# Transposing v and h in a decoder layer: TensorE identity products or transposing DMAs with ScalarE plane copies

## The chip, the cores and the metric

The kernel runs on one core of a Trainium2 chip. The metric is the device time of one execution in microseconds (us); a kernel's time is the median of its runs. A profile is one further execution, recorded by the hardware profiler; durations of single instructions come from it.

The engines of the core are named as the profile names them: PE (TensorE, matrix products), PEld (its weight loads), DVE (VectorE), ACT (ScalarE), POOL (GpSimd) and SP (SyncE, which here issues nearly all transfers). Each engine works through its own instructions in a fixed order. SBUF is the on-chip memory with 128 partitions, PSUM the accumulators that PE writes.

## The reference

One layer of a decoder trunk over 1024 prompt tokens and 8 sample tokens, with 1024 features, all in fp32:

```python
xn = _rmsnorm(x, pre_g)
u, v, z_a, x_b, z_b, g_a, g_b = split(xn @ w_in)
vn = _layernorm(gelu(v), ln_g, ln_b)                  # per token, over the features
y_a = gelu(u) * _chunk_spatial_mix(vn, w_s, b_s) * silu(z_a)   # mixes the 128 tokens of a chunk
y_b = pool_branch(x_b) * silu(z_b)
m = sigmoid(g_a) * (y_a @ w_pa) + sigmoid(g_b) * (y_b @ w_pb)
h = h + _rmsnorm(m @ w_out, post_g)
e = p @ w_ple
gate = sigmoid(_rmsnorm(h, ple_in_g) @ w_pg)
h = h + _rmsnorm(gate * e, ple_out_g)
```

The change touches two places. v comes out of its product with the features on the partitions, and the layer norm and the mix want tokens there. h comes out of the product with W_out with the tokens on the partitions, and the product with W_pg, which contracts over features, wants features there.

## The kernel before

**Products.** Each large product runs in four pairs of 128-row blocks, and each pair as seven smaller products, P1 to P7, over quarters of the operands (Strassen and Winograd's scheme; only pair 0 of v is done as four plain steps). The operands on the right are quarters and sums of quarters: B11, B21 and B22 are quarters, T1 to T4 sums. The names in the trace put the operand's letter ahead (`xB11h`, `woT1h`, `wgB22l`), and `h` and `l` at the end are the two parts of an fp32 value, since every fp32 product is three matmuls: high by high, high by low, low by high. ACT makes the high part by a copy (`split`), DVE the low part by a subtraction. A product of one quarter is 12 matmuls of 512 columns in PSUM. There are three PSUM regions of two banks for these sums (`acc`, `acct`) and two single banks for all else (`vt`, `pht`, `mix`). P5 and P3 use the same region: P3 adds onto what P5 left there, so P3 can't begin before DVE has read P5's sum.

**Stages** in the order of time: v, the gate g_A, u and z_a, x_b and z_b with the pooling, the gate g_B, the products with W_pa and W_pb, the product with W_out (`outsteps`, whose tiles are `mw`, `wo...` and `h`), and the product with W_pg (`gatesteps`, whose tiles are `hw`, `wg...` and `ge`).

**Order.** The program records all operations first (`Planner.take`) with a due time counted back from the matmul that needs them, and an estimate of each one's duration (`Planner.duration`). `Planner.order` then works out one fixed order for each engine, and `play` issues it. So all instructions after the first few carry one line number, that of `play` (L293, and L297 after the change), and they are told apart by their tiles. `at(step, f)` hangs an operation to a step of seven; a larger step number means later.

**v.** `v_turn` transposes two token blocks of a pair of v at a time: four products with the identity on PE into a bank `vt`, from which ACT takes the gelu and writes it into `big`, an SBUF tile with tokens on the partitions, adding up each row on the way (`vsums`). There are 64 such 128 x 128 transposes and 8 small ones for the 8 sample tokens. The layer norm (`ln_stats`, `ln_apply`) and the mix (`v_split`, `spatial`) follow in the stage of g_A.

**h.** `out_finish(t)` scales a block of 128 tokens by its norm and adds the layer's input by an accumulating DMA of POOL, then stores it. `gate_norm(t)` takes the sum of squares (ACT), the root (POOL), and multiplies h by it (DVE) into `hn`. `gate_input(t)` transposes `hn` by eight products with the identity into two banks `pht`, and eight ACT copies take them into `big`, each scaled by its feature's gain `ple_in`. There are 64 such transposes. The products with W_pg then read `big` as the left operand (`hw`, `hs`).

**W_pg** is prepared during the stage of x_b and z_b: `column_steps` and `column_sums` load its row blocks and store the sums of quarters to DRAM (`wglow`, `wghigh`, `wgT4`, `wgB22`); the plain quarters B11 and B21 are loaded later from the weight itself.

Of the kernel before, what the change touches and what calls it, by code (L numbers as in the profile page):

```python
# [8 lines left out]
F32 = mybir.dt.float32  # L9
F32R = mybir.dt.float32r  # L10
BF16 = mybir.dt.bfloat16
AF = mybir.ActivationFunctionType
ALU = mybir.AluOpType

P = 128
# [39 lines left out]
class Planner:  # L55
# [25 lines left out]
    def space(self, ap):  # L81

        dims, start = list(ap.ap), ap.offset
        if "DRAM" in str(ap.space):
            row = ap.tensor.shape[-1]
            first, start = divmod(start, row)
            rows = sum(s // row * (n - 1) for s, n in dims if s >= row)
            return (ap.tensor.name, first, first + rows + 1,
                    ((start, start + sum(s * (n - 1) for s, n in dims if s < row) + 1),))
        row, parts = dims[0]  # L90
        first, start = divmod(start, row)
        pieces = [(start, start + 1)]
# [35 lines left out]
    def duration(self, engine, method, out, reads, kwargs):  # L128
# [9 lines left out]
        if engine == "scalar":  # L138
            return max(0.09 + n * 0.00086, 0.26 if n > 1 else 0) + (0.2 if kwargs.get("accum_out") is not None else 0)
        return 0.1 + n * 0.0008 if method == "memset" else 1.0  # L140

    def take(self, engine, method, args, kwargs):
# [14 lines left out]
        if method == "dma_start":  # L157
            op.busy, op.moved = 1.0 if engine == "gpsimd" else 0.45, writes[0].size() * 4e-6
# [141 lines left out]
def hybrid_step(  # L300
# [82 lines left out]
    def root(part, n=P):  # L383

        t, r = sm("ms"), sm("rstd")
# [470 lines left out]
    S = NB  # L856
    xop = Operand("x")
# [7 lines left out]

    def v_turn(out, pair, ts):

        if ts == [S]:
# [3 lines left out]
            places = [(S, ps[:NS, : 2 * P], NS)]  # L872
        else:
            ps = bank("vt").rearrange("p (t c) -> p t c", t=2)
# [3 lines left out]
            places = [(t, ps[:, i], P) for i, t in enumerate(ts)]  # L878
        for t, src, n in places:
            nc.scalar.activation(out=vtok(t)[:n, 2 * pair * P : (2 * pair + 2) * P], in_=src,  # L880
                                 func=AF.Gelu_apprx_tanh, accum_out=vsums[:n, t, pair : pair + 1])

    class V(User):
        turns = [[0, 1], [2, 3], [4, 5], [6, 7], [S]]
# [113 lines left out]
    wgcut = {what: dram.tile([HALF, D], F32, tag="wg" + what, name="wg" + what) for what in ('T4', 'B22')}  # L998
    kept["h"] = dram.tile([T, D], F32, tag="h", name="h")
# [262 lines left out]
    for i, u in enumerate(vusers):  # L1262

        nxt = vsteps[1][3:] if i == 0 else (vsteps[i + 1][1:] if i + 1 < NPAIR else gasteps[0][0:])
        if i == 0:
            nxt = vsteps[1][2:]
        for s, ts in zip(nxt, V.turns):
            at(s, lambda u=u, i=i, ts=ts: v_turn(u.out, i, ts))
# [53 lines left out]
    rows = lambda t: NS if t == S else P  # L1322
# [4 lines left out]
    def column_sums(key, src, b):  # L1327
# [25 lines left out]
    column_steps("wg", w_pg, [(bflow[9 + 7 * i], bflow[12 + 7 * i]) for i in range(4)])  # L1353
# [12 lines left out]
    h_of, parts, hn_of, samples = {}, {}, {}, {}  # L1366
# [36 lines left out]

    def gate_norm(t):

        r = rows(t)
        h = h_of.pop(t)
        hn = hn_of[t] = slot("hn", (P, D))
        rs = rstd([square_sum(h[:r], r, scratch=hn)], r)
        nc.vector.tensor_scalar_mul(hn[:r], h[:r], rs[:r])  # L1410

    def gate_input(t):

        hn = hn_of.pop(t)
        if t == S:
            samples["h"] = sample_stationary(hn, NB, gvec[:, 2 * NB :])
# [296 lines left out]
```

## Time and profile before

| | before |
|---|---|
| time, median of 3 runs | 1001.62 us (1001.23 to 1002.43) |
| span of the profiled execution | 1002.0 us |
| DVE busy | 800.1 us (80%) in 1241 instructions |
| ACT busy | 490.0 us (49%) in 891 instructions |
| POOL busy | 73.7 us (7%) in 162 instructions |
| mean granted clock of TensorE | 0.996 |

The profile has no other time of its execution than the span, which stands within the range of the three runs. A row of a group reads: line, engine, operation, out<-in by the program's names (numbers left out), shapes, count | busy time, mean duration in ns of one | idle time of the engine ahead of them and what ended most of it. A row of the timeline reads: start in us, duration, engine, operation, names, count, and in brackets the idle time ahead of it with its releaser. Consecutive instructions of an engine overlap in these durations, so the cost of one in a row of many is the distance between two starts. A row of the windows gives the busy time of PE, PEld, DVE, ACT and POOL in a stretch of time, then the granted clock, the share of the 16 DMA engines, and GB/s.

### The profile page before, as it was taken

How to read it: one execution, taken by the hardware profiler on the slowest of the kernel's cores; microseconds unless marked ns; L12 is line 12 of the kernel's file. 1: busy time of each engine (PE TensorE's matmuls, PEld its weight loads, DVE VectorE, ACT ScalarE, POOL GpSimd, SP SyncE). 2: the span in 40 equal slices, each digit the busy share in tenths (PEclk: the TensorE clock that was granted, in tenths of full speed). 3: DMA queues.
4: the chain of work that ended last, by engine and by line, in shares of the span. 5: the costliest groups of instructions: out<-in, count | busy, mean ns of one | idle time of the engine just before them, and what ended most of it. 6: DMA issues, size and time to landing. Idle time of an engine off the chain costs nothing.

```text
span 1002.0 us, 16159 instructions
## 1 busy us (share of the span) xinstructions
PE 989.1 (99%) x6200; PEld 889.8 (89%) x6200; DVE 800.1 (80%) x1241; ACT 490.0 (49%) x891; POOL 73.7 (7%) x162
## 2 busy tenths in 40 slices
PE   8999999999999999999999999999999999999996
PEld 7889999999999999999999999999999988888885
DVE  5985448877788788788898887697799798779796
ACT  7664356556434343233433343552353365677653
POOL 2200001000000000000000100000000002312111
PEclk9999999999999999999999999999999999999998
DMA  9231214222364345637544166884573553389546
GB/s 353 117 121 43 84 43 129 85 85 86 101 235 169 127 167 183 210 127 252 200 158 143 61 222 244 266 305 148 199 268 107 177 201 71 80 275 364 160 109 188
DMA packets 87330, 166.95 MB, mean 167 GB/s; under 512 B 7614, under 2 KB 47598, under 8 KB 87245
## 3 DMA queue, kind: packets, MB, share of 16 engines
q1 hardware_dynamic: 84885, 158.01, 45.3%
q0 software_dynamic: 2048, 7.37, 4.3%
q8 instruction: 49, 0.80, 0.3%
q10 hardware_dynamic: 320, 0.54, 0.2%
q14 instruction: 28, 0.23, 0.1%
HBM read 114.59 MB, written 51.77 MB: 166 GB/s over the span
## 4 chain that ended last, share of the span: by engine, by line
PE 97%; DVE 1%; POOL 0%; issue 0%; ACT 0%; POOLq 0%; DVEq 0%
PE acc L293 71%; PE acct L293 15%; PE accm L293 2%; PE e L293 2%; PE sps L293 2%; PE mix L293 1%; PE vt L293 1%; PE pst L293 1%; PE pht L293 1%; PE warm L293 1%; DVE sv L293 0%; DVE ge L293 0%; PE smix L293 0%; PE state L293 0%; DVE welo L293 0%
## 5 line engine op out<-in xcount | busy, mean ns | idle before, releaser
L293 DVE TENSOR_TENSOR u<-acc,u 128x520 f32<-128x520 f32 (+1 forms) x90 | 62.5, 695 | 36.5 <-PE acc L293 35.0
L293 POOL TENSOR_TENSOR rstd<-ms,mhalf 128x1 f32<-128x1 f32 (+1 forms) x45 | 38.2, 851 | 204.8 <-DVE ms L293 182.5
L293 POOL MEMSET u<- 128x8 f32 x35 | 3.5, 105 | 556.1 <-PE acc L293 242.5
L293 ACT ACTIVATE u<-acc 128x512 f32<-128x512 f32 x39 | 23.2, 596 | 33.4 <-PE acc L293 33.1
L293 ACT ACTIVATE paw<-pas 128x512 fp32r<-128x512 f32 x16 | 10.0, 627 | 30.0 <-DVE pas L293 24.8
L293 ACT ACTIVATE pbw<-pbs 128x512 fp32r<-128x512 f32 x16 | 10.0, 629 | 29.1 <-DVE pbs L293 25.9
L293 DVE TENSOR_TENSOR big<-big 128x1024 f32<-128x1024 f32 (+4 forms) x20 | 23.6, 1215 | 0.0
L293 ACT ACTIVATE big<-vt 128x256 f32<-128x256 f32 x32 | 11.9, 380 | 21.4 <-PE vt L293 21.4
L293 ACT ACTIVATE big<-pht,gvec 128x128 f32<-128x128 f32 x64 | 18.0, 381 | 8.0 <-PE pht L293 8.0
L293 ACT ACTIVATE big<-mix 128x256 f32<-128x256 f32 x32 | 12.1, 383 | 19.0 <-PE mix L293 18.6
L293 PE MATMUL accm<-qh,wpoolw 128*128 128x260 f32 (+1 forms) x96 | 21.0, 320 | 0.0
L293 ACT ACT_TABLE_LOAD x13 | 16.7, 1283 | 4.6 <-PE acc L293 3.6
L293 DVE TENSOR_TENSOR v<-acc,u 128x520 f32<-128x520 f32 (+1 forms) x9 | 6.3, 697 | 14.9 <-PE acc L293 14.8
L293 DVE TENSOR_TENSOR acc<-acc,u 128x512 f32<-128x512 f32 (+1 forms) x16 | 11.1, 697 | 8.7 <-PE acc L293 8.7
L293 ACT ACTIVATE gbw<-gbs 128x512 fp32r<-128x512 f32 x16 | 10.0, 624 | 16.4 <-DVE gbs L293 13.8
L293 ACT ACTIVATE zaw<-zas 128x512 fp32r<-128x512 f32 x16 | 10.0, 628 | 14.9 <-DVE zas L293 10.6
L293 ACT ACTIVATE zbw<-zbs 128x512 fp32r<-128x512 f32 x16 | 10.1, 630 | 14.6 <-DVE zbs L293 7.3
L293 PEld LDWEIGHTS accm<-qh,wpoolw 128*128 128x128 f32 x96 | 15.5, 188 | 1.9
L293 DVE TENSOR_TENSOR big<-mix,big 128x256 f32<-128x256 f32 x32 | 13.2, 421 | 4.4 <-ACT big L293 3.5
L293 ACT ACTIVATE uw<-us 128x512 fp32r<-128x512 f32 x16 | 9.8, 627 | 13.7 <-DVE us L293 7.2
L293 ACT ACTIVATE zbw<-zbraw 128x512 fp32r<-128x512 f32 x12 | 7.5, 626 | 18.2 <-DMA zbraw<-in_w_in_dram 9.2
L293 ACT ACTIVATE gb<-gb 128x1032 f32<-128x1032 f32 (+1 forms) x8 | 6.8, 854 | 18.8 <-DVE gb L293 18.8
(687 smaller groups left out, 3629.8 us busy)
## 6 DMA issues: line engine op xcount, KB each, us to landing
ga<-ga SPq DMA_DIRECT2D x16, 516.0 KB
gb<-gb SPq DMA_DIRECT2D x16, 516.0 KB
ya<-za SPq DMA_DIRECT2D x8, 516.0 KB
yb<-zb SPq DMA_DIRECT2D x8, 516.0 KB
x<-in_x_prompt_dram SPq DMA_DIRECT2D x8, 512.0 KB
vraw<-in_w_in_dram SPq DMA_DIRECT2D x8, 512.0 KB
e<-e SPq DMA_DIRECT2D x8, 512.0 KB
garaw<-in_w_in_dram SPq DMA_DIRECT2D x8, 512.0 KB
```

The lines of the kernel that those rows point to most:

```text
L293: getattr(getattr(self.nc, e), method)(*args, **kwargs)
```

## The change

The 64 transposes of v and the 64 of h on PE go; only those of the sample tokens stay.

**v.** `v_planes` takes the two 16-bit halves of each fp32 value of a block apart: two ACT copies (one for the low halves, one for the high ones) write them into a tile `vw` of 16-bit words, all low halves of a row first, then all high ones. A transposing DMA of SP writes `vw` back into the slot of `v`, turned in 128 x 128 blocks of words. `v_join` puts the halves together again, two ACT copies for each block, each for four token blocks, into `big`. `v_turn` then takes the gelu from `big` into `big`.

**h.** `gate_norm` no longer multiplies h by the root. It takes the sum of squares (its squares go into `big`, where they are not used), keeps the root in a column of `vsums` (`rin`), and sends raw h through the same steps: two ACT copies into `hw`, one transposing DMA into the slot of h. `gate_input` joins by two ACT copies. The root enters later as the scale of the sigmoid in `gated`, and the gain `ple_in` goes into W_pg: `column_sums` scales its row blocks on ACT (8 copies of 128 x 1024) and stores their left halves to DRAM (`wgleft`), from which B11 and B21 are then loaded.

The layer norm's steps are hung two steps later, those of W_pg's columns one step earlier. The planner gets durations for the 16-bit copies and handles regions in bytes. GpSimd takes no part in the transposing.

```diff
+    def v_planes(out, pair):
+        for m in range(2):
+            words, v = slot("vw", (P, 2, SEQ), U16), out[m][:, :SEQ].bitcast(U16)
+            for w in range(2):
+                nc.scalar.activation(out=words[:, w], in_=v.rearrange("p (t w) -> p w t", w=2)[:, w], func=AF.Copy)
+            nc.sync.dma_start_transpose(out=v.rearrange("p (k c) -> p k c", c=P),
+                                        in_=words.rearrange("p w t -> p (w t)"))
+
+    def v_join(out, pair, m):
+        c = 2 * (2 * pair + m) * P
+        for j in range(2):
+            ts = slice(4 * j, 4 * j + 4)
+            nc.scalar.activation(out=big.bitcast(U16)[:, ts, c : c + 2 * P].rearrange("p t (c w) -> p t c w", w=2),
+                                 in_=out[m][:, :SEQ].bitcast(U16).rearrange("p (w t c) -> p t c w", w=2, c=P)[:, ts],
+                                 func=AF.Copy)
...
-            for i, t in enumerate(ts):
-                for m in range(2):
-                    nc.tensor.transpose(ps[:, i, m * P : (m + 1) * P], out[m][:, t * P : (t + 1) * P], ident)
...
+            nc.scalar.activation(out=v, in_=ps[:NS, : 2 * P] if t == S else v, func=AF.Gelu_apprx_tanh,
+                                 accum_out=vsums[:n, t, pair : pair + 1])
     class V(User):
-        turns = [[0, 1], [2, 3], [4, 5], [6, 7], [S]]
+        turns = [[7, 0, 1], [2, 3, 4], [5, 6]]
...
-        nxt = vsteps[1][3:] if i == 0 else (vsteps[i + 1][1:] if i + 1 < NPAIR else gasteps[0][0:])
...
+        nxt = vsteps[1][1:] + vsteps[2] if i == 0 else (vsteps[i + 1] if i + 1 < NPAIR else gasteps[0])
+        at(nxt[0], lambda u=u, i=i: v_turn(u.out, i, [S]))
+        at(nxt[0], lambda u=u, i=i: v_planes(u.out, i))
+        for m in range(2):
+            at(nxt[2 + m], lambda u=u, i=i, m=m: v_join(u.out, i, m))
+        for s, ts in zip(nxt[4:], V.turns):
+            at(s, lambda i=i, ts=ts: v_turn(None, i, ts))
...
-        s = 3 + 4 * n
+        s = 5 + 4 * n
...
+            for i, t in enumerate(raw if cuts else ()):
+                nc.scalar.activation(out=t, in_=t, func=AF.Copy, scale=col(2, 4 * i + b))
+                dma(kept["wgleft"][(4 * i + b) * P : (4 * i + b + 1) * P, :], t[:, :HALF])
...
-    column_steps("wg", w_pg, [(bflow[9 + 7 * i], bflow[12 + 7 * i]) for i in range(4)])
+    column_steps("wg", w_pg, [(bflow[8 + 7 * i], bflow[11 + 7 * i]) for i in range(4)])
...
     def gate_norm(t):
...
-        rs = rstd([square_sum(h[:r], r, scratch=hn)], r)
-        nc.vector.tensor_scalar_mul(hn[:r], h[:r], rs[:r])
...
+        nc.scalar.activation(out=spare, in_=src, func=AF.Square, scale=D ** -0.5, accum_out=n[:r])
+        root(n, r, rin(t))
...
+        words = slot("hw", (P, 2, D), U16)
+        for w in range(2):
+            nc.scalar.activation(out=words[:, w], in_=h.bitcast(U16).rearrange("p (c w) -> p w c", w=2)[:, w], func=AF.Copy)
+        h_of[t] = h.bitcast(U16).rearrange("p (k t) -> p k t", t=P)
+        nc.sync.dma_start_transpose(out=h_of[t], in_=words.rearrange("p w c -> p (w c)"))
 
     def gate_input(t):
...
-        for k4 in range(0, NB, 4):
-            ps = bank("pht")
-            for k in range(4):
-                nc.tensor.transpose(ps[:, k * P : (k + 1) * P], hn[:, (k4 + k) * P : (k4 + k + 1) * P], ident)
-            for k in range(4):
-                nc.scalar.activation(out=big[:, k4 + k, t * P : (t + 1) * P], in_=ps[:, k * P : (k + 1) * P],
-                                     func=AF.Copy, scale=col(2, k4 + k))
+        for k in (slice(0, 4), slice(4, NB)):
+            nc.scalar.activation(out=words_of(t)[:, k].rearrange("p k (t w) -> p k t w", w=2),
+                                 in_=got.rearrange("p (w k) t -> p k t w", w=2)[:, k], func=AF.Copy)
...
-        nc.scalar.activation(out=g, in_=src, func=AF.Sigmoid)
+        nc.scalar.activation(out=g, in_=src, func=AF.Sigmoid, scale=rin(t))
...
-    woop, wgop = stored("wo", w_out, HALF), stored("wg", w_pg, HALF, split=wgcut)
+    woop, wgop = stored("wo", w_out, HALF), stored("wg", kept["wgleft"], HALF, split=wgcut)
```

The planner's order moves with it. **ACT in the stage of v**, at the second pair, before the change: `vw` are parts of the weights (here not the 16-bit tile), `u` and `v` evacuations of PSUM, and the gelus read `vt`.

```order
L293 ACTIVATE u_184_307<-acc_183_306 128x512
L293 ACTIVATE vw_190_313<-vs_176_299 128x512
L293 ACTIVATE sv_12_109,vsums_108<-vt_181_304 8x256
L293 ACTIVATE vw_194_317<-vs_177_300 128x512
L293 ACTIVATE big_96,vsums_108<-vt_189_312 128x256 x2
L293 ACTIVATE vw_197_320<-vraw_185_308 128x512
L293 ACTIVATE v_191_314<-acc_183_306 128x512
L293 ACTIVATE big_96,vsums_108<-vt_193_316 128x256 x2
```

The same place of ACT after the change: the rows of 128 x 1024 from `v` are the plane copies, those of 128 x 4 x 256 the joins.

```order
L297 ACTIVATE u_182_306<-acc_181_305 128x512
L297 ACTIVATE vw_180_304<-vs_177_301 128x512
L297 ACTIVATE vw_190_314<-vs_176_300 128x512
L297 ACTIVATE vw_162_286<-v_96_215 128x1024 x2
L297 ACTIVATE vw_193_317<-vs_177_301 128x512
L297 ACTIVATE vw_184_308<-v_164_288 128x1024 x2
L297 ACTIVATE sv_12_109,vsums_108<-vt_183_307 8x256
L297 ACTIVATE big_96<-v_96_215 128x4x256
L297 ACTIVATE v_191_315<-acc_181_305 128x512
L297 ACTIVATE vw_195_319<-vraw_186_310 128x512
L297 ACTIVATE big_96<-v_96_215 128x4x256
```

The join of `v_96` stands behind only three groups of copies that follow its planes, and the evacuation of the region `acc_181` (product P2) and the next part of the weights stand behind that join.

**PE at the end of the stage of v**, before the change, from the last product T1 (P5) of the last pair; `acc_234` with `gaw` is the first product of g_A. Between P5 and the product B22 (P3) on the same region `acc_230` stand transposes and that product.

```order
L293 MATMUL acc_230_353<-xT1h_139_262,vw_217_340 128x260 x2
L293 MATMUL vt_226_349<-ident_72,v_191_314 128x128
L293 MATMUL vt_226_349<-ident_72,v_192_315 128x128
...
L293 MATMUL vt_231_354<-ident_72,v_191_314 8x128
L293 MATMUL vt_231_354<-ident_72,v_192_315 8x128
L293 MATMUL acc_234_357<-xB11h_71_189,gaw_224_347 128x512
L293 MATMUL acc_234_357<-xB11l_72_190,gaw_224_347 128x512
...
L293 MATMUL acc_230_353<-xB22h_111_229,vw_221_344 128x260 x2
```

The same place of PE after the change.

```order
L297 MATMUL acc_225_349<-xT1h_139_263,vw_215_339 128x260 x2
L297 MATMUL acc_225_349<-xB22h_111_230,vw_218_342 128x260 x2
L297 MATMUL acc_225_349<-xB22l_112_231,vw_218_342 128x260 x2
...
L297 MATMUL acc_225_349<-xB22h_113_232,vw_218_342 128x260 x2
L297 MATMUL acc_228_352<-xB11h_71_190,gaw_220_344 128x512
```

P3 now stands directly behind P5 on the region `acc_225`, and g_A's first product behind both. The same neighbourhood of P5 and P3 arises once more, at the last pair of the product with W_out.

**DVE at the end of the product with W_out**, before the change: `h_1308` is the last block of h, `acct_1318` holds its P5, `acct_1307` its P4, the `wg...l` are low parts of W_pg and the `hw` parts of the left operand.

```order
L293 TENSOR_TENSOR u_1266_1397<-acct_1299_1430,u_1266_1397 128x512
L293 TENSOR_TENSOR wgT2l_1301_1432<-wgT2_1279_1410,wgT2h_1300_1431 128x1024
L293 TENSOR_SCALAR hn_1281_1412<-h_1251_1382,rstd_1284_1415 128x1024
L293 TENSOR_TENSOR wgT2l_1303_1434<-wgT2_1280_1411,wgT2h_1302_1433 128x1024
L293 TENSOR_TENSOR hw_1315_1446<-hs_1316_1447,hw_1315_1446 128x512
L293 TENSOR_TENSOR hw_1330_1461<-big_96,hw_1330_1461 128x512
L293 TENSOR_TENSOR h_1308_1439<-acct_1318_1449,u_1266_1397 128x512
L293 TENSOR_TENSOR h_1308_1439<-acct_1307_1438,u_1266_1397 128x512
```

The same place of DVE after the change, where the block is `h_1285`, P5 is in `acct_1295` and P4 in `acct_1284`.

```order
L297 TENSOR_TENSOR wgB11l_1270_1402<-wgB11_1246_1378,wgB11h_1269_1401 128x1024
L297 TENSOR_TENSOR h_1285_1417<-acct_1295_1427,u_1245_1377 128x512
L297 TENSOR_TENSOR wgB11l_1272_1404<-wgB11_1247_1379,wgB11h_1271_1403 128x1024
L297 TENSOR_TENSOR wgT2l_1278_1410<-wgT2_1258_1390,wgT2h_1277_1409 128x1024
L297 TENSOR_TENSOR wgT2l_1280_1412<-wgT2_1259_1391,wgT2h_1279_1411 128x1024
L297 TENSOR_TENSOR h_1285_1417<-acct_1284_1416,u_1245_1377 128x512
```

Three low parts now stand between the two reads. The first product with W_pg takes, as the next of the three regions, the one that the second read frees.

More of the change, by code (lines that the diff above doesn't have):

```diff
@@ L81, in space @@
     def space(self, ap):
-        dims, start = list(ap.ap), ap.offset
+        size = 2 if ap.dtype in (BF16, U16) else 4
+        dims, start = [(s * size, n) for s, n in ap.ap], ap.offset * size
         if "DRAM" in str(ap.space):
-            row = ap.tensor.shape[-1]
+            row = ap.tensor.shape[-1] * size
             first, start = divmod(start, row)
@@ L138, in duration @@
         if engine == "scalar":
-            return max(0.09 + n * 0.00086, 0.26 if n > 1 else 0) + (0.2 if kwargs.get("accum_out") is not None else 0)
+            return max(0.09 + n * (0.00101 if out.dtype == U16 else 0.00086), 0.26 if n > 1 else 0) + (0.2 if kwargs.get("accum_out") is not None else 0)
+        if method == "tensor_copy":
+            return 0.15 + n * 0.0011
         return 0.1 + n * 0.0008 if method == "memset" else 1.0
@@ L156, in take @@
         op.spent.append(op.busy)
-        if method == "dma_start":
-            op.busy, op.moved = 1.0 if engine == "gpsimd" else 0.45, writes[0].size() * 4e-6
+        if method[:9] == "dma_start":
+            op.busy, op.moved = 1.0 if engine == "gpsimd" else 0.45, writes[0].size() * (2e-6 if writes[0].dtype == U16 else 4e-6)
             op.lands = 4.5 if kwargs.get("accum_op") is not None else 2.0
@@ L856, in hybrid_step @@
     S = NB
+    rows = lambda t: NS if t == S else P
     xop = Operand("x")
```

41 lines of the change are left out of this document (20 added, 21 removed).

## The prediction

> **What bounds the kernel now.** I read the page first, then the chain of work that ended last, then windows over the two stages that the change touches.
>
> ```profile
> span 1002.0 us, 16159 instructions
> PE 989.1 (99%) x6200; PEld 889.8 (89%) x6200; DVE 800.1 (80%) x1241; ACT 490.0 (49%) x891; POOL 73.7 (7%) x162
> PE 97%; DVE 1%; POOL 0%; issue 0%; ACT 0%; POOLq 0%; DVEq 0%
> 80.00:100.00 20.00, 20.00 (x137) 18.30 (x136) 10.25 (x16) 9.96 (x34) 0.00 (x0) 1.00 0.17 54
> 100.00:120.00 20.00, 20.00 (x139) 18.53 (x138) 9.16 (x15) 7.49 (x24) 0.00 (x0) 1.00 0.31 106
> 120.00:140.00 20.00, 20.00 (x147) 18.71 (x145) 9.44 (x16) 8.02 (x26) 0.10 (x1) 1.00 0.16 53
> 860.00:880.00 20.00, 20.00 (x97) 16.18 (x96) 14.46 (x27) 13.43 (x36) 5.73 (x8) 1.00 0.50 109
> 880.00:900.00 20.00, 20.00 (x97) 16.45 (x96) 14.41 (x21) 15.64 (x37) 3.46 (x5) 1.00 0.93 281
> 900.00:920.00 20.00, 20.00 (x97) 16.48 (x96) 18.00 (x25) 16.34 (x38) 5.36 (x5) 1.00 1.05 378
> ```
>
> PE is 99% busy and 97% of the chain. In the windows of v (80 to 140 us) and of h (860 to 920 us) PE is busy for 20.00 of 20 us at a granted clock of 1.00. So nothing but PE's own work sets the time there, and PE work taken away is time gained, as long as nothing else becomes late. ACT is the engine to watch: 10.0, 7.5 and 8.0 of 20 us in v, but 13.4 to 16.3 of 20 in h.
>
> **What goes from PE.** Two groups, and the timeline around one block of each:
>
> ```profile
> L293 PE MATMUL vt<-ident,v 128*128 128x128 f32 x64 | 9.5, 273 | 0.0
> L293 PE MATMUL pht<-ident,hn 128*128 128x128 f32 x64 | 8.3, 273 | 0.0
> ...
> 120.57 0.60 PE L293 MATMUL vt<-ident,v 128*128 128x128 f32 x4
> 120.92 0.48 PE L293 MATMUL acc<-xT3h,vw 128*128 128x260 f32 x2
> 121.24 0.41 PE L293 MATMUL acc<-xT3l,vw 128*128 128x260 f32 x2
> 121.49 0.64 PE L293 MATMUL acc<-xT3h,vw 128*128 128x260 f32 x4
> ...
> 858.06 0.40 PE L293 MATMUL acct<-woT1h,mw 128*128 128x512 f32 x1
> 858.29 1.03 PE L293 MATMUL pht<-ident,hn 128*128 128x128 f32 x8
> 859.08 0.48 PE L293 MATMUL acct<-woB11h,mw 128*128 128x512 f32 x1
> 859.40 0.39 PE L293 MATMUL acct<-woB11l,mw 128*128 128x512 f32 x1
> ```
>
> The groups' busy time (17.8 us) counts ends that overlap, so I take distances between starts. Eight transposes of h last from 858.29 to 859.08, 0.79 us, and the first matmul behind takes 0.32 instead of 0.23 us (858.06 to 858.29): 0.88 us a block, 8 x 0.88 = 7.0 us. Four transposes of v last from 120.57 to 120.92, 0.35 us, and the pair of matmuls behind takes 0.32 instead of the 0.25 of the next pair: 0.42 us. The order has the 64 of v as fourteen blocks of four and one of eight, 14 x 0.42 + 0.88 = 6.8 us. Together **13.8 us** leave PE.
>
> **What comes to ACT.**
>
> ```profile
> L293 ACT ACTIVATE vh<-big 128x1024 fp32r<-128x1024 f32 x8 | 8.5, 1058 | 11.3 <-DVE big L293 11.3
> 889.50 2.04 ACT L293 ACTIVATE wgB11h<-wgB 128x1024 fp32r<-128x1024 f32 x2
> 891.40 0.66 ACT L293 ACTIVATE big<-pht,gvec 128x128 f32<-128x128 f32 x2
> 880.95 2.18 ACT L293 ACTIVATE big<-pht,gvec 128x128 f32<-128x128 f32 x8 [0.24 <-PE pht L293]
> 882.96 0.68 ACT L293 ACTIVATE junk<-h 128x512 bf16<-128x512 f32 x1
> 500.00:550.00 50.00, 50.00 (x335) 46.04 (x334) 44.35 (x68) 18.66 (x30) 3.35 (x11) 1.00 0.44 152
> ```
>
> A copy of 1024 elements shows 1058 ns, and two in a row cost 891.40 - 889.50 = 1.90, so 0.95 us each. Each of the 16 blocks now has four such copies (two planes, two joins), 3.8 us. In 16-bit words with a stride of two, no row shows them. Bounds: 0.95 us if only the count of elements matters, 1.9 if the stride halves the rate. I take 0.95, that of the nearest rows, which are copies of the same count; the planner's own figure in the diff is a little higher (0.00101 against 0.00086 us an element).
>
> For v these are 32 x 0.95 = 30.4 us more on an ACT that was busy for 25.5 of the 60 us of the three windows. From the first plane to the last join ACT's rows come to some 57 us, in 68 us of PE's work, so some 11 us are spare. For h the eight copies from PSUM go, 882.96 - 880.95 = 2.0 us, and 3.8 come: +1.8 a block, 14 us over a stage of 100 us in which ACT was 67 to 82% busy. It still fits. The eight scalings of W_pg (7.6 us) lie in the stage of x_b, where ACT is busy for 18.7 of 50 us; without that cover they would cost 7.6. The eight DVE products `hn` go, and two table loads come on ACT; neither engine is the bound, so I count both as nothing.
>
> **What ACT waits for.** In the order of ACT each join stands in line, and until the transposing DMA has landed everything behind it stands too: the evacuations of PSUM that free PE's regions, and the next weights' high parts. No transposing DMA is in this trace, so its time L from issue to landing is bounded by plain and by accumulating ones of the same 512 KB:
>
> ```profile
> 114.67 0.35 SPq L293 DMA_DIRECT2D lnb<-in_ln_b_dram  x1
> DMA  9999999997521053988957100000000000000000
> ...
> h<-in_x_prompt_dram POOLq DMA_DIRECT2D x8, 512.0 KB, 7.3
> ...
> 108.38 0.63 ACT L293 ACTIVATE vw<-vraw 128x512 fp32r<-128x512 f32 x1 [3.48 <-PE acc L293]
> 108.92 0.37 ACT L293 ACTIVATE big<-vt 128x256 f32<-128x256 f32 x1
> 109.63 0.36 ACT L293 ACTIVATE sv<-vt 8x256 f32<-8x256 f32 x1
> 109.99 0.61 ACT L293 ACTIVATE vw<-vs 128x512 fp32r<-128x512 f32 x1
> ```
>
> The lone load at 114.67 moves its data in the slices from 115.5 to 117.75 (the second row cuts 112 to 122 us into 40): L = 3.1 at least. POOL's accumulating transfers land after 7.3 in the median, the upper bound. I take **L = 5**, between the two, as a transposing one does more than a plain and reads no second operand.
>
> What ACT does meanwhile is its cover. For block 1 of pair 0 of v that is a 512-wide copy (108.92 - 108.38 = 0.54), two planes (1.9) and a sample gelu (109.99 - 109.63 = 0.36): 2.8 us. Worked out in the same way, the eight blocks of v have 1.1, 2.8, 9, 4.2, 3.7, 6.2, 5.8 and 4.7 us. At L = 5 ACT stands for 3.9 + 2.2 + 0.8 + 1.3 + 0.3 = 8.5 us in v, inside the 11 spare. At 7.3 it stands for 22.6, 11.6 too many. The eight blocks of h have 4.0, 4.0, 7.5, over 8 three times, 3.5 and 2.3: 1.0 + 1.0 + 1.5 + 2.7 = 6.2 us at L = 5, 15.4 at 7.3, against some 14 spare. So v decides, and the point from which PE is held up as a whole lies near **L = 5.5 to 7**. Because spare time isn't spread evenly (the wait at pair 0 stands ahead of P2's evacuation), I charge 1.5 us at L = 5.
>
> SP has 16 transposing DMAs and 8 stores more to issue, and loads behind a transposing DMA wait for its planes. Loads come many us ahead (the DMA share in v is 0.16 to 0.31), so I count nothing; in h the share is 0.93 to 1.05, which speaks for a longer L there.
>
> One rule speaks against the change. The Trainium skill, "VectorE: DVE Perf Modes", section "The three transpose paths", gives 390 ns for a 128 x 128 transpose by TensorE and 1309 ns by DMA; sixteen of those in a row would make L an estimated 20.9 us, and by the waits above the kernel would take over 1040 us. The same skill, "DMA: Bandwidth & Descriptors", section "Latency and other measured facts", states 261 GB/s for transposing DMAs, an estimated 2.0 us for 512 KB, by which all would be hidden. This trace shows a 128 x 128 transpose on PE at 273 ns, and no transposing DMA.
>
> **New neighbours on PE.** The transposes also stood as filling between products. The order now has, twice, P3 directly behind P5 on the same region (end of v, end of W_out), and DVE must read in between.
>
> ```profile
> L293 DVE TENSOR_TENSOR v<-acc,u 128x520 f32<-128x520 f32 x6 | 4.2, 699 | 13.4 <-PE acc L293 13.4
> L293 DVE TENSOR_TENSOR h<-acct,u 128x512 f32<-128x512 f32 x12 | 8.1, 686 | 2.5 <-PE acct L293 2.3
> 891.34 2.35 DVE L293 TENSOR_TENSOR wgB11l<-wgB,wgB11h 128x1024 fp32r<-128x1024 f32 x2
> 893.61 0.68 DVE L293 TENSOR_TENSOR hw<-big,hw 128x512 fp32r<-128x512 f32 x1
> ```
>
> Each costs the last matmul's end (0.40 busy less 0.23 of distance, 0.17), the read (0.69 or 0.70) and two hand-overs between engines, which no row shows alone and which I estimate at 0.2: 1.05, twice 2.1 us. Then the first product of W_pg needs the region that DVE's second read frees, and ahead of that read stand three low parts at (893.61 - 891.34) / 2 = 1.13 us. From P5's read: 3 x 1.13 + 0.69 + 0.4 of hand-overs = 4.5, against P3's 12 x 0.23 = 2.8: **1.7 us** of waiting.
>
> **The sum.** 1002.0 - 13.8 + 2.1 + 1.7 + 1.5 = 993.5 for a profiled execution. The span of before stands 0.4 above the median of its runs, so the predicted time is 993.1 us.
>
> **Rivals.**
> - *All is hidden*: L near 3.1, and DVE is ahead of its order, so that only the two waits of 1.05 stay, or not even these: 986 to 990. For it speak the spare ACT time and the low DMA share in v; against it the order's new neighbours.
> - *ACT becomes the bound of v*: 16-bit copies cost more than 0.95 us. Each 0.1 us more adds 32 x 0.1 = 3.2 us in v; with 8.5 us of waits, the 11 spare are gone at once. At 1.15 us, 6.4 - 2.5 = 4 us are lost, 997; at 1.3, 11.2 - 2.5 = 9, so 1002; at the bound of 1.9, 28 us, 1021. For it speaks the planner's figure (0.15 us more in 1024 elements), against it that every ACT copy in these rows goes by its count.
> - *Slower*: the transposing DMA is what ACT stands behind. Place: the joins of v, above all pair 0 with its covers of 1.1 and 2.8. At L = 7.3 the sum is 1002.0 - 13.8 + 2.1 + 1.7 + 1.5 + 11.6 - 0.4 = 1004.7; it decides from L near 7, and each further us costs some 7. For it speaks that these move 2-byte words, that blocks of a pair go out together, and the rule above.
> - *That the change doesn't do what it says* is out: the order has 128 transposes fewer on PE.
>
> **How the numbers follow.** The forecast (990 to 997) has a chance of 0.48, all hidden 0.18, ACT the bound 0.18 (997 to 1003), slower 0.16. The smallest difference that a measurement of this kernel can tell from none is about 0.2%, 2 us, so "same" is 999.6 to 1003.6. The first two cases and 0.07 of ACT's lie below, 0.73; the other 0.11 of ACT's is within; above lies 0.16. The range goes from 986.5, the lower end of all hidden, to 1005, the upper bound of L; beyond stay a longer L and copies near 1.9 us.
>
> **What would show it.** PE with about 6070 matmuls and no `vt` of 128 rows nor `pht`; at the last P3 of v and of W_out, PE idle for about 1 us behind DVE's `v` and `h`, and some 2 us ahead of the first `wgB11h`. Planes and joins near 0.95 us each. ACT's waits on DMA at the joins summing to some 8 us in v; if they sum to over 20, the third rival is right, and PE is then seen idle between 80 and 150 us behind ACT. I'd be wrong in another way if PE stood idle in the last 100 us for weights of W_pg, whose loads share the queue with the transposing DMAs.

## The result, and the profile after

| | before | after |
|---|---|---|
| time, median of 6 runs | 1002.02 us (1001.23 to 1003.68) | 1015.75 us (1005.70 to 1018.65) |
| ratio to before, 95% interval | | 1.0119 (1.0098 to 1.0141) |
| span of the profiled execution | 1002.0 us | 1015.4 us |
| ACT busy | 490.0 us | 550.5 us |
| mean granted clock of TensorE | 0.996 | 0.990 |

The kernel became slower by 1.2%, where 993.1 us and a gain were forecast. The time of an execution of the changed kernel includes 1.7 to 1.8 us beyond its span (1017.2 for this one), in one of the six some 3 us, so the forecast's step from span to median (0.4 us) was not exact, which is small here. The runs after the change also spread over 13 us, those of before over 2.5. The ratios of this document leave out a run that is over 1.5% above the fastest of its kernel, which is one of the four of `h_alone` below (1018.90 us is the median of the other three) and no other.

The page after, with the lines that answer to those shown of before: span, busy times, and the packets of the DMA queues, of before (the first of the packet lines) and after.

```profile
span 1015.4 us, 15943 instructions
PE 982.0 (97%) x6072; PEld 877.7 (86%) x6072; DVE 793.9 (78%) x1231; ACT 550.5 (54%) x901; POOL 72.8 (7%) x162
```

```profile
DMA packets 87330, 166.95 MB, mean 167 GB/s; under 512 B 7614, under 2 KB 47598, under 8 KB 87245
```

```profile
DMA packets 121760, 177.41 MB, mean 175 GB/s; under 512 B 41022, under 2 KB 81006, under 8 KB 121677
```

PE has its 128 transposes fewer. The packets under 512 bytes grew by 33408, that is 2088 for each of the 16 transposing DMAs of 512 KB, so they move in pieces of about 256 bytes. (The second number of the packet lines is the traffic; the 10.5 MB more of traffic are the 16 transfers, 8.4 MB, and W_pg's left halves.)

Where the time goes is read from the first and the last matmul of the stage of W_pg, in the view of the tile `hw`; behind the durations in ns (smallest, median, largest) stand the first and the last start. First before, then after:

```profile
L293 PE MATMUL acct<-wgB11h,hw x32: 388/394/483, 902.3 to 973.3; 128*128 128x512 f32 x32
L293 PE MATMUL acct<-wgB21h,hw x40: 274/390/397, 911.6 to 992.9; 128*128 128x512 f32 x24, 128*128 128x256 f32 x16
```

```profile
L297 PE MATMUL acct<-wgB11h,hw x32: 387/393/497, 898.5 to 985.6; 128*128 128x512 f32 x32
L297 PE MATMUL acct<-wgB21h,hw x40: 279/390/502, 906.7 to 1006.0; 128*128 128x512 f32 x24, 128*128 128x256 f32 x16
```

Up to that stage the changed kernel is 3.8 us ahead. In it, it needs 107.5 us in place of 90.6, so **16.9 us are lost in the last stage alone**. The windows of that stage after the change, with the columns of the windows above:

```profile
900.00:920.00 20.00, 17.04 (x71) 12.67 (x70) 15.45 (x24) 16.98 (x28) 3.89 (x5) 1.00 1.08 354
920.00:940.00 20.00, 10.13 (x44) 7.88 (x43) 7.89 (x13) 7.31 (x10) 0.88 (x1) 0.82 0.89 132
940.00:960.00 20.00, 19.27 (x72) 15.48 (x73) 12.89 (x23) 14.18 (x25) 6.01 (x6) 0.84 0.81 223
```

From 920 to 940 us PE is busy for 10.13 of 20 us, and DVE and ACT for under 8, while the DMA engines are busy for 0.89 of the time at a mere 132 GB/s: everybody waits for transfers that move slowly. The granted clock is 0.82 from 920 to 940 us and 0.84 from 940 to 960; in the latter PE is busy again for 19.27 us, and 19.27 x 0.16 = 3.1 us of them are an estimate of what the lower clock costs there. PE's longest waits in the stage, from its timeline, with the releaser in brackets:

```profile
906.72 0.50 PE L297 MATMUL acct<-wgB21h,hw 128*128 128x512 f32 x1 [2.55 <-ACT u L297]
940.73 0.79 PE L297 MATMUL acct<-wgB22l,hw 128*128 128x512 f32 x1 [10.60 <-DMA wgB22l<-wgB]
979.11 0.50 PE L297 MATMUL acct<-wgT1h,hw 128*128 128x512 f32 x1 [1.92 <-ACT ge L297]
```

The longest is for a plain load, the last piece of `wgB22l`. Behind it stands SP's queue, in which the load is the row after two transposing DMAs of h:

```profile
911.19 8.85 SPq L297 DMA_TRANSPOSE h<-hw  x1
920.32 5.28 SPq L297 DMA_TRANSPOSE h<-hw  x1
935.98 0.37 SPq L297 DMA_DIRECT2D wgB22l<-wgB  x1
```

SP is held for 8.85 and 5.28 us issuing the two, and issues the load only 10.4 us after that. The cause of that second delay is in the waits of the order: the load's destination slot is the one that held the second DMA's 16-bit tile, and it comes free when that DMA has landed. ACT stood for these two as well, first a copy that takes the slot of the first one's tile, then the join of the second block:

```profile
924.14 0.63 ACT L297 ACTIVATE hw<-big 128x512 fp32r<-128x512 f32 x1 [5.43 <-DMA h<-hw]
...
935.95 1.17 ACT L297 ACTIVATE big<-h 128x1024 uint16<-128x1024 uint16 x1 [8.55 <-DMA h<-hw]
```

So the first of the two lands 924.14 - 911.19 = 13 us after its issue, and the second 935.95 - 920.32 = 15.6 us after its own. In the stage of v, one that has the queue to itself, with the copy on ACT that waits for it (issue at 105.96; the second fence cuts 105 to 125 us into 40 slices of half a us):

```profile
105.96 1.80 SPq L297 DMA_TRANSPOSE v<-vw  x1
110.32 0.63 ACT L297 ACTIVATE vw<-vraw 128x512 fp32r<-128x512 f32 x1 [0.35 <-DMA v<-vw]
```

```profile
DMA  0000799992000000000000000000069999979999
GB/s 0 0 0 0 144 212 214 216 208 54 0 0 0 0 0 0 0 0 0 0 0 0 0 0 0 0 0 0 0 125 214 215 216 199 172 199 303 363 371 348
```

Its data move from 107.1 to about 109.7, 2.6 us, at 214 GB/s, and ACT goes on 4.4 us after its issue. By the updates of their semaphores in the trace, the eight transposing DMAs of v land 3.7 to 6.8 us after their issues, 5.0 in the mean. The same view over 905 to 945 us, one slice a us, where the two of h move:

```profile
DMA  9999999999999919979999699974300079999999
GB/s 397 401 416 397 406 406 404 404 393 385 395 428 384 148 27 274 255 131 201 190 245 120 77 104 54 49 79 85 77 18 4 0 135 197 348 352 410 426 410 393
```

Up to 918 the queue is full of plain transfers, mostly W_pg's, at some 400 GB/s; the transposing ones wait behind them. From 926 to 932 the DMA engines are busy for 0.6 to 0.9 of the time but move only 49 to 120 GB/s. What moves from the landing of the first transposing DMA to that of the second (924.1 to 936 us) are two queues, POOL's accumulating transfers (`software_dynamic`; packets, MB, share of the time) and the second transposing DMA (`hardware_dynamic`):

```profile
q0 software_dynamic: 164, 0.56, 44.7%
q1 hardware_dynamic: 2063, 0.52, 42.8%
```

Those 1.08 MB take 11.3 us. Alone, the transposing DMA of v above moved its 0.52 MB in 2.6 us, and an accumulating transfer, the only one to move from 991 to 995 us, its 0.52 MB in 3.5. So here the two kinds slow each other: single packets of the accumulating transfers take up to 3.5 us there, and 1.0 at most from 991 to 995.

The copies on ACT cost nearly what was assumed:

```profile
L297 ACT ACTIVATE vw<-v 128x1024 uint16<-128x1024 uint16 x16 | 16.1, 1042 | 0.0
L297 ACT ACTIVATE big<-v 128x1024 uint16<-128x1024 uint16 x16 | 18.5, 1173 | 8.0 <-DMA v<-vw 8.0
L297 ACT ACTIVATE big<-h 128x1024 uint16<-128x1024 uint16 x16 | 18.5, 1174 | 20.4 <-DMA h<-hw 20.4
```

A plane copy is as long as an fp32 copy of the same count (1058 ns), a join, which reads the two planes by turns, 11% longer. ACT stands for 8.0 us at v's joins, and for 20.4 at h's; with the copies that wait for a slot of the 16-bit tile it is 28.0 for h.

### The profile page after: what moved, and what is told of

It is laid out like the page before. It is cut to its first block, busy times and chain, and to the rows that moved or that the text cites. A ratio compares the mean times of both kernels' runs of the same rounds, so it can differ in the third digit from the quotient of the medians.

```text
span 1015.4 us, 15943 instructions
## 1 busy us (share of the span) xinstructions
PE 982.0 (97%) x6072; PEld 877.7 (86%) x6072; DVE 793.9 (78%) x1231; ACT 550.5 (54%) x901; POOL 72.8 (7%) x162
## 5 line engine op out<-in xcount | busy, mean ns | idle before, releaser
L297 POOL TENSOR_TENSOR rstd<-ms,mhalf 128x1 f32<-128x1 f32 (+1 forms) x36 | 30.6, 851 | 222.4 <-DVE ms L297 222.3
L297 ACT ACTIVATE big<-h 128x1024 uint16<-128x1024 uint16 (+1 forms) x24 | 26.7, 1132 | 20.4 <-DMA h<-hw 20.4
L297 ACT ACTIVATE big<-v 128x1024 uint16<-128x1024 uint16 x16 | 18.5, 1173 | 8.0 <-DMA v<-vw 8.0
L297 DVE TENSOR_TENSOR hw<-hs,hw 128x512 fp32r<-128x512 f32 x16 | 10.8, 681 | 11.7 <-ACT hw L297 11.7
L297 PEld LDWEIGHTS accm<-qh,wpoolw 128*128 128x128 f32 x96 | 15.6, 188 | 1.9
L297 DVE TENSOR_TENSOR mw<-ms,mw 128x512 fp32r<-128x512 f32 x16 | 11.0, 687 | 8.0 <-ACT mw L297 7.9
L297 PE MATMUL acct<-wgB22l,hw 128*128 128x512 f32 x16 | 6.9, 433 | 10.6 <-DMA wgB22l<-wgB 10.6
```

Of the source, the lines that this page charges most:

```text
L297: getattr(getattr(self.nc, e), method)(*args, **kwargs)
```

## The experiments

Two theories stood at the start. **Queue theory**: the loss is h's alone; its transposing DMAs land late among W_pg's loads and hold up the loads behind them. **ACT theory**: ACT's standing at the joins, and its copies, cost in both stages. Each kernel was compared with the kernel before on the same chip, whose median there was 1002.2 to 1002.8 us. Edits are against the changed kernel unless said.

**v_alone** takes h's part back, with W_pg's scaling.

```diff
-        h_of[t] = h.bitcast(U16).rearrange("p (k t) -> p k t", t=P)
-        nc.sync.dma_start_transpose(out=h_of[t], in_=words.rearrange("p w c -> p (w c)"))
+        rs = rstd([square_sum(h[:r], r, scratch=hn)], r)
+        nc.vector.tensor_scalar_mul(hn[:r], h[:r], rs[:r])
...
```

> Only v goes by planes, transposing DMA and joins; h and W_pg are as before the change. Queue theory (the loss comes from h's transposing DMAs, which hold up the last loads of W_pg behind them): v's part is a gain, 6.8 us of PE less the waits of 1.0 and 0.3 us that the changed kernel shows in v, so 996 to 998.5. ACT theory (ACT standing at the joins costs in both stages): ACT stood for 8.0 us at v's joins, and with copies of 1.04 and 1.17 us in place of 0.95 little of the gain is left: 1000 to 1004.

Measured: 999.84 us (997.42 to 1001.79, 10 runs), ratio 0.9975 (0.9965 to 0.9985). Faster than before by 2.8 us of the 6.8; the time lies between the two expectations, nearer to the second. In its profile W_out's first product starts at 806.8 us against 811.9 before, and after the set-up of the first 11 us PE waits only at three places, 2.0 us together:

```profile
126.85 0.51 PE L297 MATMUL acc<-xB22h,vw 128*128 128x260 f32 x2 [1.12 <-DVE v L297]
134.15 0.74 PE L297 MATMUL acc<-xT2h,gaw 128*128 128x260 f32 x4 [0.33 <-DVE gaw L297]
324.98 0.50 PE L297 MATMUL acc<-xB11h,zaw 128*128 128x512 f32 x1 [0.53 <-DVE u L297]
```

The profile of before has a granted clock of 0.91 from 160 to 180 us, which costs it 1.8 us and is not in that of v_alone: 5.1 - 1.8 = 3.3 us is what v's part is worth there, near the 2.8 of the medians.

**h_alone** takes v's part back.

```diff
-        nxt = vsteps[1][1:] + vsteps[2] if i == 0 else (vsteps[i + 1] if i + 1 < NPAIR else gasteps[0])
+        nxt = vsteps[1][3:] if i == 0 else (vsteps[i + 1][1:] if i + 1 < NPAIR else gasteps[0][0:])
...
```

> Only h and W_pg as in the change; v is as before. Queue theory: the whole loss is here, so the changed kernel's 1015.8 plus the 4 to 5 us that v's part gives, 1014 to 1021, with PE idle for some 10 us on wgB22l, its last load. ACT theory: half of it, 1005 to 1010.

Measured: 1023.52 us (1015.56 to 1030.89, 4 runs), ratio 1.0185 (1.0126 to 1.0244). The whole loss and more is in h, with the same wait on `wgB22l`, 9.4 us, and one of 11.3 us on DVE's `ge` at 975 us. The queue theory held, and the ACT theory fell in its form of an equal loss in both stages. That ACT's standing at h's joins costs nothing is not shown: in the changed kernel the wait of PE at 979.11 (1.92 us, behind ACT's `ge`) follows a join that stood for 5.85 us.

**late_landing** lets the planner count on a late landing.

```diff
-            op.lands = 4.5 if kwargs.get("accum_op") is not None else 2.0
+            op.lands = 4.5 if kwargs.get("accum_op") is not None else 12.0 if method != "dma_start" else 2.0
```

> One number of the planner changes: it counts 12 us and not 2 from the transposing DMA's transfer to its landing. In SP's order the last load of wgB22 then stands ahead of the transposing DMAs of the third pair of h, and no longer takes the slot that the last of them frees. Queue theory: the wait of 10.6 us goes, and with it the lower clock behind it; the time falls to 995 to 1003. ACT theory: the joins stand later in ACT's order too, but the copies stay; under 5 us are gained, 1010 to 1016.

Measured: 1048.31 us (1047.13 to 1049.30), ratio 1.0458 (1.0443 to 1.0474). A miss for both. ACT hardly stands at h's joins any more (0.7 us, and 4.2 at a copy that waits for a slot), and the wait on `wgB22l` is gone, but the whole order moved, also where no transfer was late. PE's waits add up to 39 us; the longest lies in v:

```profile
112.11 1.23 PE L297 MATMUL acc<-xT3h,vw 128*128 128x260 f32 x4 [7.06 <-DVE vw L297]
```

It says that a plan with a landing of 12 us everywhere is worse than one with too short a landing, and nothing on what makes the landing long.

**no_x** leaves out POOL's accumulating DMA of x, so h lacks x.

```diff
-        nc.gpsimd.dma_start(out=h, in_=x_of(t), accum_op=ALU.add)
```

> Leaves out POOL's accumulating DMA of x into h after W_out, so h lacks x. It asks why h's transposing DMAs land so late (14 and 10 us at 911 to 936) when those of v take about 4. If they share the DMA engines with the accumulating transfers and lose by it: every one of h's lands within 6 us of its issue, and the wait on wgB22l falls under 3 us; 995 to 1003. If it is the queue of plain loads ahead of them alone: the third pair's still take over 10 us and the wait stays above 6 us.

Measured: 997.01 us, a single run, so without an interval. PE's waits fall to 6.1 us in all, none on `wgB22l`, and ACT stands for 3.5 us at h's joins. So the loss depends on the accumulating DMA. But without it h is also ready earlier, and the planner's order differs: traffic and chain are not yet apart.

**own_words** gives the 16-bit tile a buffer of its own.

```diff
-SLOTS = 46
+SLOTS = 45
...
-        words = slot("hw", (P, 2, D), U16)
+        words = hwords[t % 1]
```

> The 16-bit tile of h gets one buffer of its own, and the shared slots go from 46 to 45. So no load of W_pg can inherit the tile's slot, and in SP's order all loads of wgB22 stand ahead of the transposing DMAs of the third pair. The accumulating DMAs and the chain of h stay. Slot theory (the 10.6 us of PE come from wgB22l waiting for the slot that a transposing DMA frees): that wait is gone, 1000 to 1006, with the landing of h's transposing DMAs still 10 us or more. Contention theory (the DMA queues are full and W_pg's loads are late in any order): the wait moves to another load or to the joins and the time stays at 1010 or above.

Measured: 1033.93 us (1031.75 to 1036.62), ratio 1.0313 (1.0293 to 1.0333). It doesn't decide: with one slot fewer, and one buffer that all eight blocks of h share, PE waits elsewhere (10.0 us at 503 us in the pooling mixes). But the wait on `wgB22l` is gone, and one of the same size has come at another place, behind DVE's `h`:

```profile
930.26 0.79 PE L297 MATMUL acct<-woB22h,mw 128*128 128x512 f32 x1 [10.37 <-DVE h L297]
```

**x_aside** keeps the accumulating traffic and takes it out of h's chain, so h lacks x here too.

```diff
-        nc.gpsimd.dma_start(out=h, in_=x_of(t), accum_op=ALU.add)
+        aside = slot("aside", (P, D))
+        nc.gpsimd.memset(aside, 0.0)
+        nc.gpsimd.dma_start(out=aside[:r], in_=x_of(t), accum_op=ALU.add)
```

> POOL's accumulating DMA of x stays, with its bytes and its place, but goes into a tile of zeros that nobody reads, so h lacks x and does not wait for it. Against the run without that DMA (997.0) it differs by the traffic alone. If the accumulating transfers slow the transposing ones: h's third and fourth pair land 8 us or more after their issue and the time is above 1003. If it is the 7 to 10 us that the accumulating DMA adds to the chain of each h block: 996 to 1000, as without it.

Measured: 1005.42 us (1002.66 to 1007.02, 8 runs), ratio 1.0029 (1.0019 to 1.0040). Of the 18.7 us between the changed kernel and no_x, 8.4 come back with the traffic (and with a memset, a slot more for each block, and the order that follows), and about 10 belong to h's readiness and its order. The time is that of the first expectation, but its sign is missing: in the profile next to nothing accumulates beside the transposing DMAs of the last two pairs, and by their semaphores they land in 3.7 to 6.2 us. So the 8.4 us are not the price of the two kinds meeting; PE's longest waits in W_pg's stage are 2.4 us for the load of `wgT4h` and 1.8 behind ACT's `u`.

**x_plain** loads x plainly, ahead of time, and adds it on DVE.

```diff
-        nc.gpsimd.dma_start(out=h, in_=x_of(t), accum_op=ALU.add)
+        add(h, h, xin.pop(t)[:r])
...
+        at(outsteps[i][5], lambda ts=ts: [x_back(t) for t in ts])
```

> h gets x by a plain load that is issued ahead and an addition on DVE, in place of POOL's accumulating DMA; the result is the same. Chain or contention, both go: 996 to 1001, faster than before the change if the slot isn't taken again. If only the slot matters, it stays above 1005, since the last load of wgB22 still stands behind one transposing DMA in SP's order.

Measured: 999.43 us (997.22 to 1004.62, 10 runs), ratio 0.9974 (0.9959 to 0.9990), faster than both kernels. The change as a whole is a gain once the accumulating DMAs are out of h's way.

**v_order** is v_alone with another order in the last pair of v.

```diff
+        vsteps.append(strassen(w, xop, u, order=("P1", "P6", "P2", "P7", "P5", "P4", "P3")) if i == NPAIR - 1
+                      else (strassen if i else classical)(w, xop, u))
```

> v alone as in the first run, with the last pair of v in the order P1, P6, P2, P7, P5, P4, P3, so that P4 stands between P5 and P3 on their region. The wait of 1.1 us at that P3 goes: 1.0 us under v alone, 998.0 to 999.5, if PE's waits are what is lost of the 6.8 us of transposes; equal to v alone (999.8) if the wait only moves to the next product.

Measured: 1000.22 us (997.87 to 1000.92, 11 runs), ratio 0.9974 (0.9965 to 0.9983). The wait of 1.1 us at P3 is gone from the timeline and the time is that of v_alone: nothing gained, as three smaller waits on g_A's weights came in its place (0.40, 0.26 and 0.31 us).

**plain_copy** puts a plain DMA in the place of the transposing one of h, so h's blocks stay untransposed. Order, bytes, slots and waits stay, row by row.

```diff
-        nc.sync.dma_start_transpose(out=h_of[t], in_=words.rearrange("p w c -> p (w c)"))
+        nc.sync.dma_start(out=h.bitcast(U16), in_=words.rearrange("p w c -> p (w c)"))
```

> In h alone the transposing DMA becomes a plain one: the same 512 KB from the 16-bit tile into the slot of h, in the same row of SP's order, with the same waits and the same slots, so the joins read words that are not transposed (h's blocks are left untransposed). If it is the transposing transfer itself (its many small packets, which fill the queue and hold SP, and its slow landing beside other traffic): each lands within 5 us, the wait of PE on wgB22l falls under 2 us and the time to 995 to 1002. If any DMA in that place, with its slot handed to the next load, does the same: 1008 to 1016, with the wait above 6 us.

Measured: 999.11 us (997.62 to 999.63, 6 runs), ratio 0.9965 (0.9952 to 0.9978): 16.6 us under the changed kernel. SP's queue at the same place, the copy on ACT that waits for the first of the two, and PE's wait on the same load:

```profile
905.53 0.47 SPq L297 DMA_DIRECT2D h<-hw  x1
914.58 0.47 SPq L297 DMA_DIRECT2D h<-hw  x1
918.31 0.36 SPq L297 DMA_DIRECT2D wgB22l<-wgB  x1
```

```profile
915.77 0.63 ACT L297 ACTIVATE hw<-big 128x512 fp32r<-128x512 f32 x1 [2.34 <-DMA h<-hw]
```

```profile
925.80 0.50 PE L297 MATMUL acct<-wgB22l,hw 128*128 128x512 f32 x1 [0.48 <-DMA wgB22l<-wgB]
```

Each plain DMA holds SP for 0.47 us, in place of 8.85 and 5.28. (Between the two SP stands until the store of the second block of h has landed.) The first lands 915.77 - 905.53 = 10.2 us after its issue, nearly as late as the transposing one with its 13 us, since the same transfers stand ahead of it, and so misses the 5 us that were expected. The second makes the difference: the load still waits for its slot and goes out at 918.31, 3.7 us after that DMA's issue, where it was 15.7. So the load is out 17.7 us earlier, and PE's wait falls from 10.60 to 0.48. This is the run that settles it: the same slots, queue places, bytes and waits cost nothing as long as the transfer doesn't transpose. It does not part what comes with the transposing form: the many small packets, the long issue, and the turning itself.

**hold5** gives the load another slot.

```diff
+        if t in (5,):
+            nc.gpsimd.memset(hwords[t][:, 0, :2], 0)
```

> A small memset on POOL touches the 16-bit tile of one block of the third pair again after its join, so that the planner hands the last load of wgB22 another slot; that load stays behind the two transposing DMAs in SP's order but no longer waits for one of them to land. If the slot makes the wait of 10.6 us: it falls by 4 to 10 us and the time to 1003 to 1010. If the full queue makes it (SP held while it issues the transposing DMAs, and their packets ahead of the load's): the wait stays within 3 us of 10.6, 1012 to 1018.

Measured: 1014.32 us (1013.13 to 1018.20, 4 runs), ratio 1.0126 (1.0100 to 1.0153). The load is issued right behind the two transposing DMAs, and PE no longer waits for it, but the time is that of the changed kernel, so neither expectation held as a whole. In its profile the waits in W_pg's stage are many and smaller, 12.3 us together; the longest:

```profile
908.27 0.50 PE L297 MATMUL acct<-wgB21h,hw 128*128 128x512 f32 x1 [3.31 <-ACT u L297]
922.45 0.50 PE L297 MATMUL acct<-wgT1l,hw 128*128 128x512 f32 x1 [2.39 <-DVE wgT1l L297]
959.14 0.50 PE L297 MATMUL acct<-wgB22h,hw 128*128 128x512 f32 x1 [3.31 <-DVE ge L297]
```

The one at 959.14 stands behind a join of ACT that itself stood for 4.2 us for a transposing DMA. So the slot explains where PE stood, not that it stood.

**v_order_x** is v_order with x loaded plainly, h by PE. Its edits are those of v_order and of x_plain together.

> v by transposing DMAs with the order of the seventh run, h by PE as before the change, and x by a plain load and DVE's addition instead of POOL's accumulating DMA. It asks what h's transposing DMAs are worth once the accumulating ones are gone (999.4 with both). If they still cost more than the 7 us of PE that they free: 996 to 999. If they are worth something there: 1000 to 1004, since DVE's eight additions come on top.

Measured: 1005.35 us (1003.64 to 1007.55, 10 runs), ratio 1.0025 (1.0014 to 1.0037). DVE's additions and the extra loads, with the order that follows, cost 5.1 us against v_order. Against x_plain it is 5.9 us slower: without accumulating DMAs, h's transposing DMAs give 5.9 of the 7.0 us that they take from PE.

**h_early** sends only the first two pairs of h through the DMA.

```diff
-        if t == S:
+        if t == S or t >= 4:
             return
         words = slot("hw", (P, 2, D), U16)
```

> All as in the change, but the blocks of the last two pairs of h go through PE again (eight transposes of raw h into a bank, and two ACT copies in place of eight); only v and the first two pairs of h, whose transposing DMAs lie at 850 to 895 us, ahead of W_pg's loads, use the DMA. If the loss comes from transposing DMAs among W_pg's loads and the accumulating DMAs: v's 2.8 us and up to 3.5 of the four early blocks are gained and no long wait is left, 995.5 to 999. If each transposing DMA of h costs something wherever it stands: 1002 to 1009, about half of the changed kernel's loss.

Measured: 1004.13 us (1000.69 to 1007.44, 12 runs), ratio 1.0018 (1.0003 to 1.0033). A miss for the narrow form of the queue theory: against v_alone the four early blocks don't gain 3.5 us but lose 4.3. The time lies in the range of the second expectation, though 1.7 us over the kernel before are far from half of the loss. Its SP timeline shows that not all is well at 886 us either, where W_pg's first loads stand ahead:

```profile
875.24 1.96 SPq L297 DMA_TRANSPOSE h<-hw  x1
886.25 9.97 SPq L297 DMA_TRANSPOSE h<-hw  x1
```

PE's waits in W_pg's stage are only 2.5 us in that profile, so what the four blocks cost was not traced to its end.

## Why the prediction was wrong, point by point

- **What bounds it, and what leaves PE**: PE bounds the kernel, and the transposes left. The size was near for h (5.9 of 7.0 us are gained without accumulating DMAs, as the difference of v_order_x and x_plain) and too high for v: 3.3 us in the profiles against 6.8 less 2.0 of waits. The missing 1.5 us were not traced.
- **ACT's copies**: right. 0.95 us was taken; the distance of two planes is 0.95 (1.99 - 1.04), that of two joins 1.07 (2.24 - 1.17). ACT did not become the bound.
- **ACT's waits in v**: right in mechanism and size. 8.5 us were worked out at L = 5, and 8.0 were measured at the joins and 1.5 at other copies, with landings of 3.7 to 6.8 us, 5.0 in the mean.
- **The failing step**: one L for both stages. The text said that the DMA share of 0.93 to 1.05 in h "speaks for a longer L there", and yet counted 6.2 us of waits in h at L = 5, inside ACT's spare time, and for SP "I count nothing". In h three of the eight landed 13 to 15.6 us after their issues (those of 884.14, 911.19 and 920.32), and ACT's waits came to 28.0 us in place of 6.2. A late landing cost what the sum had no term for: the weights' loads behind them in SP's queue, and with that PE itself, 10.6 us at once. The sentence on how it could be wrong named this (PE idle for weights that share the queue), but gave it neither price nor chance.
- **The slower rival** had the right culprit, the transposing DMA, and the wrong place: v's joins. There all went as forecast, while h's blocks, counted as covered by up to 8 us, were the ones that broke. The upper bound of L, 7.3 us, came from a median over calm and crowded transfers; a median bounds nothing, and in the crowd of 880 to 900 us of before those transfers already took 8.7.
- **New neighbours**: the two waits at P3 came as forecast, 1.04 us in v and 0.88 at W_out, against 1.05 each. Less the 0.17 of the last matmul's end and the read, that leaves 0.17 and 0.02 us for the two hand-overs, which were estimated at 0.2 without a row that shows them. The 1.7 us ahead of `wgB11h` did not show; the first wait of that stage came at `wgB21h`, 2.55 us, behind ACT.
- **The rule on the price of a DMA transpose**: the 1309 ns for a 128 x 128 block in the Trainium skill, "VectorE: DVE Perf Modes", section "The three transpose paths", does not hold for blocks in a row here; sixteen of them took about 2.6 us in v. The 261 GB/s of the Trainium skill, "DMA: Bandwidth & Descriptors", section "Latency and other measured facts", are nearer: 214 GB/s measured, alone. Neither says what it does among other traffic.

What is shown: that the transposing form of h's transfers costs the loss (plain_copy, 16.6 us), and that the loss is gone when POOL's accumulating DMAs are left out or replaced (no_x, x_plain), which changes h's readiness and the order as well. That the two kinds slow each other is seen in the changed kernel's trace, from 924 to 936 us (11.3 us for what took 2.6 and 3.5 apart). x_aside can't say what that is worth, as the two hardly meet there. How much of the loss is this slowing, how much SP's long issues, and how much h's lateness stays open. Why single executions spread from 1005.7 to 1018.7 us was not traced either.

## What to carry to other kernels

A transfer's landing time is a property of the place: take it from the most crowded window in which the new transfer will stand, not from a lone one, and price what stands behind it in its queue, not only who waits for its data. Ahead of moving work from a busy engine to "free" DMA, look for the stage in which the queue is already full. To tell the kind of a transfer from its place, swap it for a plain one of the same bytes with the order unchanged.

## What the runs showed of the hardware

- A transposing DMA of 512 KB in 2-byte words moves in some 2088 packets of about 256 bytes, at 214 GB/s (105.96, alone) where plain loads reach 400, and its issue holds SP for 1.8 us in place of 0.47 for a plain one of the same bytes.
- From 924 to 936 us a transposing and an accumulating DMA, with 1.08 MB between them, took 11.3 us, where 0.52 MB of each took 2.6 and 3.5 us alone.
- The issue of a transposing DMA behind a full queue held SP for 8.9 us (911.19) and 9.7 us (884.14); a plain one of the same bytes at the same place held it for 0.47 us (plain_copy, 905.53).
- ACT copies 16-bit words that it reads with a stride of two as fast as fp32 (1042 ns for 1024), and is 11% slower where it reads two planes by turns.
- The granted clock fell to 0.82 and 0.84 in the windows around PE's longest wait; in plain_copy, without the wait, it is 1.00 there.
